# A hybrid encoder layer: the first two projection blocks in turns of 256 tokens, their weights loaded between the first tiles of x, and the sums of squares of kk later in their block

## The chip, the cores and the metric

The kernel runs on one core of one Trainium2 chip. The metric is the device time of one execution in microseconds (us), the median over several runs. The core has five engines with a queue each: TensorE (PE, matrix products, with its own row PEld for loading the stationary operand), VectorE (DVE), ScalarE (ACT), GpSimd (POOL) and SyncE (SP), which here issues the DMA transfers. An engine takes its instructions in the order in which the program gave them.

## The reference, cut to what matters

One layer runs on 1024 prompt tokens and 256 sample tokens of width 1024, so on T = 1280 tokens in all, in float32:

```
u = rmsnorm(x, norm_mix_pre)
(hc, b_gate, c_gate, r, k, v, zf, zb, gd, gate_conv, gate_rwkv) = split(u @ w_in)
y_conv = (b_gate * conv3(c_gate * hc)) @ w_branch_a
kk = k * k_k ; kk = kk / max(norm(kk per head), 1e-12)
for d, z in ((forward, zf), (backward, zb)):
    z = z + shift_mu[d] * (z_shifted - z) ; zw, za = z[:64], z[64:]
    w = exp(-exp(-softplus(-(decay_w0 + tanh(zw) @ decay_w2)) - 0.5))
    a = sigmoid(iclr_a0 + za @ iclr_a2)
    outs[d] = scan over tokens of a 64x64 state per head (r, w, kk, kk*a, kd(k, a), v)
y = groupnorm(outs[0] + outs[1]) + bonus(r, k, r_k, v)
y_rwkv = (y * (sigmoid(gd) @ gate_g2)) @ w_branch_b
x = x + rmsnorm((sigmoid(gate_conv)*y_conv + sigmoid(gate_rwkv)*y_rwkv) @ w_out)
x = x + rmsnorm(conv_ffn(rmsnorm(x)))
x = x + rmsnorm(sigmoid(x @ w_ple_gate) * (p @ w_ple))
```

The change lies in the first lines: the norm of x, the projections zf, zb and gd of u, and the per-head norm of kk.

## The kernel before

**Split products.** Each float32 operand is kept as a high half (rounded) and a low half (the rest). A product is three matmuls: high by high, high by low, low by high (`mm3`). The high half is a cast on ACT, the low half a subtraction on DVE, or on POOL for the first two blocks of weights. Weights pass through `raw` (two buffers), then `wh` and `wl` (two each).

**First loop (lines 887 to 957).** x comes in ten tiles of 128 tokens. For tile i the loop issues the load of tile i+5; scales tile i+1 on DVE (`scale`: tile, 1/rms, gain, into `xs`); transposes tile i on PE in eight 128x128 pieces into two banks `tp`; casts these into the high half of `U` on ACT and subtracts the low half on DVE; takes the root for tile i+3 (`root`: square root on ACT, reciprocal on DVE, four small steps on POOL) and the squares of tile i+4 (`stats`: ACT squares and sums, POOL scales the sum); and then lets the fill queue run for some us of matrix work with `go`. The low and high halves of the first two blocks' weights are made in the turns i = 2 and 3. The constants' later part, the small vectors and gate_g2 are loaded on the same SP queue in the turns 2 and 6; gate_g2 is split in turn 9.

**Fill queue (class `Fill`).** All projections are blocks of 128 output columns. A block gives units: one unit is the three matmuls of one of eight pieces of the inner dimension, on up to 512 tokens (booked at 0.65 us) or 256 (0.325 us). `go(us)` takes units until their booked time is used up; `until(n)` finishes the first n blocks. The first entry is a `Pair` of the blocks zf and zb, then comes gd, then four times k and r (one pair of heads each), then v, the convolution's and the gates' blocks. When a block has given `ahead` units, the next block's weights are split, one half at each `every` units. After a group of eight units its bank `mm` is evacuated, at the first unit of the group that follows; there are two banks.

**Side jobs.** What follows a block on DVE, ACT and POOL is put on a list by its `done`, and one job is taken from it when units of more than 0.9 us (0.6 us from the k blocks on) have gone by; `run_side()` takes all. zf and zb have nine jobs each (token shift, tanh, cast and low half of zw, cast and low half of za), gd has three (scale, cast, low half). The ten products with gate_g2 (`g_out`) stand in the k block of the first head pair, after `go(3.0)` and `run_side()`, and need gd's halves.

**After the loop (lines 960 to 968)** space of the first loop is taken over by a new pool; two loads of constants go to it and to a buffer `gth`, and ACT casts two tiles (`bo`, `ind`) from them.

**Head pairs (lines 990 to 1002).** For each of four head pairs: in the k block, the small products of the pair before (`rates`: `lora` and what follows on ACT, DVE, POOL, with stores to DRAM in `d_in`); then the r block, where after 1.7 us of units kk squared is split (`halve`) and after a further lead `kk_norm` lets PE sum the squares over the head (`ones`, with `bo`), and DVE takes the maximum, four reciprocals and a product with kk. That product goes into the `rates` of the same pair, in the next k block. After the four pairs the scan begins, which reads `d_in` and `d_kr` back.

All five engines' instructions are pinned to program order by a small wrapper, whose line 199 is therefore the line of nearly all rows.

Of the kernel before, what the change touches and what calls it, by code (L numbers as in the profile page):

```python
# [18 lines left out]
TTS = ((0, 512), (512, 512), (1024, 256))  # L19
# [40 lines left out]
class B:  # L60
# [5 lines left out]
    def sb(self, pool, shape, dt=F32, tag=None, bufs=None):  # L66
        kw = {} if bufs is None else dict(bufs=bufs)
        return pool.tile(shape, dt, name=tag, tag=tag, **kw)
# [57 lines left out]
def build(tc, I, O, dbg=None, upto=99):  # L126
# [5 lines left out]
    def tok(name, i, n=1):  # L132
        if i < 8:
            return I[name + "_prompt"][0, i * 128:(i + n) * 128, :]
        return I[name + "_sample"][0, (i - 8) * 128:(i - 8 + n) * 128, :]
# [24 lines left out]
    def close(*ps):  # L160
        for p in ps:
            open_pools.pop(id(p)).__exit__(None, None, None)
# [47 lines left out]
    PADS = (1, 513, 1027)  # L210
# [6 lines left out]
    def mm3(out, st_, mv, k, last):  # L217
        (sh, sl), (mh, ml) = st_, mv
        PE.matmul(out, sh, mh, start=k == 0, stop=False)
        PE.matmul(out, sh, ml, start=False, stop=False)  # L220
        PE.matmul(out, sl, mh, start=False, stop=k == last)
# [6 lines left out]
    def side(fs):  # L228
        sides.extend(fs)

    def run_side(n=1000, qs=(soon, sides)):
        for q in qs:
            while q and n > 0:
                q.pop(0)()
                n -= 1

    class Block:

        parts, us, ahead, every = 1, 13.0, 4, 4
# [15 lines left out]
        def units(self):  # L255
            hi, lo = self.w
            if self.begin:
                self.begin()
            for (t0, n), po in zip(TTS, PADS):
                ps = sb(pmm, [128, 512], F32, "mm")[:, 0:n]  # L260
                for k in range(8):
                    mm3(ps, (hi[:, k, :], lo[:, k, :]), ucm(t0, n)(k), k, 7)
                    yield n / 512 * 0.65
                self.evac(ps, t0, n, po)
            if self.done:
                self.done()

    class Pair:

        parts, us, ahead, every = 2, 26.0, 36, 2  # L270

        def __init__(self, *blocks):
            self.blocks = blocks
# [7 lines left out]
        def units(self):  # L281
            for x in self.blocks:
                x.begin()
            for p, q in ((0, 0), (1, 0), (0, 1), (0, 2), (1, 1), (1, 2)):
                x, (t0, n), po = self.blocks[p], TTS[q], PADS[q]
                ps = sb(pmm, [128, 512], F32, "mm")[:, 0:n]
                for k in range(8):
                    mm3(ps, (x.w[0][:, k, :], x.w[1][:, k, :]), ucm(t0, n)(k), k, 7)
                    yield n / 512 * 0.65
                x.evac(ps, t0, n, po)  # L290
                if q == 2:
                    x.done()

    class VBlock:

        parts, us, ahead, every = 2, 26.0, 56, 4
# [173 lines left out]
    def ones(ps, w, hl):  # L470

        for t0, n in TTS:
            for q in range(2):
                PE.matmul(ps[:, t0:t0 + n], w, hl[q][:, t0:t0 + n], start=q == 0, stop=q == 1)
# [18 lines left out]
    def kk_norm(hp):  # L493

        ps = sb(psm, [128, 3 * 512], F32, "sm")
        ones(ps, S1["bo"], S1["sq"])
        n2 = kns[hp] = sb(p1, [128, T], F32, "t5", 3)
        V.tensor_scalar(n2, ps[:, 0:T], 1e-24, None, ALU.max)
        side([lambda t=t: V.reciprocal(n2[:, t:t + 320], n2[:, t:t + 320]) for t in range(0, T, 320)])
        side([lambda: V.tensor_tensor(n2, n2, kks[hp], ALU.mult)])  # L500
# [134 lines left out]
    class Branch:  # L635


        parts, us, ahead, every = 1, 6.4, 2, 3
# [45 lines left out]
    class Out:  # L684

        ahead, every = 4, 4
# [165 lines left out]
    fill = Fill(items, left)  # L852
    fill.early[first_out - 2] = 1
    go = fill.run
# [9 lines left out]
    def load_x0(i):  # L864
        if i < NT:
            X0[i] = sb(wq, [128, D], F32, "cvy") if i == 4 else sb(p0, [128, D], F32, "x", 5)
            SP.dma_start(X0[i], tok("x", i))

    def stats(i):
        if i < NT:  # L870
            ss = sb(p0, [128, 1], F32, "ss", 3)
            A.activation(junk, X0[i], AF.Square, accum_out=ss)
            ms = S1["ms", i] = sb(p0, [128, 1], F32, "ms", 3)
            G.tensor_scalar(ms, ss, 1.0 / D, 1e-6, ALU.mult, ALU.add)

    def root(i):
        if i < NT:
            s = S1["s", i] = sb(p0, [128, 1], F32, "s", 3)
            A.activation(s, S1["ms", i], AF.Sqrt)
            S1["rs", i] = b.newton(p0, S1["ms", i], s, 1, f"n0{i % 3}", V if i == 0 else G, V)  # L880

    def scale(i):
        if i < NT:
            S1["xs", i] = sb(p0, [128, D], F32, "xs", 2)
            V.scalar_tensor_tensor(S1["xs", i], X0[i], S1["rs", i], gmix, ALU.mult, ALU.mult)
# [2 lines left out]
    SP.dma_start(cst[:, 0:128], I["consts"][:, 0:128])  # L888
    SP.dma_start(gmix, I["norm_mix_pre"].broadcast_to((128, D)))
    load_x0(1)  # L890
    load_x0(2)
    load_x0(3)
    load_x0(4)
    junk = sb(p1, [128, D], F32, "o5", 4)
    warm = sb(p0, [128, 1], F32, "warm")
    G.memset(warm, 1.0)
    A.activation(warm, warm, AF.Sqrt)
    fill.load_next()
    half = sb(cp, [128, 24], F32, "half")
    lw = []  # L900

# [3 lines left out]
    stats(1)  # L905
    root(1)
    stats(2)
    root(2)
    stats(3)
    for i in range(NT):  # L910
        load_x0(i + 5)
        if i == 1:
            fill.load_next()
        if i == 2:
            SP.dma_start(cst[:, 128:], I["consts"][:, 128:C_EARLY])
            for name, n in (("conv_w", 12), ("conv_b", 4), ("shift_mu", 2), ("decay_w0", 8),
                            ("iclr_a0", 8), ("k_k", 4), ("k_a", 4), ("r_k", 4)):
                ap = I[name]
                flat = ap.rearrange({2: "a b -> (a b)", 3: "a b c -> (a b c)"}[len(ap.shape)])
                SP.dma_start(prow[at:at + n, :], flat.rearrange("(r p) -> r p", p=128))  # L920
                PC[name] = at
                at += n
            pc = lambda name, i: pcol[:, PC[name] + i:PC[name] + i + 1]
        scale(i + 1)
        pss = []
        for j in range(2):
            ps = sb(pt, [128, 4, 128], F32, "tp")
            for k in range(4):
                PE.transpose(ps[:, k, :], S1["xs", i][:, (4 * j + k) * 128:(4 * j + k + 1) * 128], ident)
            uh = U[:, 4 * j:4 * j + 4, 0, i * 128:(i + 1) * 128]  # L930
            A.copy(uh, ps)
            pss.append((ps, uh))
        for j, (ps, uh) in enumerate(pss):
            V.tensor_tensor(U[:, 4 * j:4 * j + 4, 1, i * 128:(i + 1) * 128], ps, uh.bitcast(F32), ALU.subtract)
        root(i + 3)
        stats(i + 4)
        if i in (2, 3):
            for _ in fill.split_next():
                pass
        if i == 6:  # L940
            ps = sb(pt, [128, 4, 128], F32, "tp")
            PE.transpose(ps[:, 0, 0:at], prow[0:at, :], ident[0:at, 0:at])
            V.tensor_copy(pcol[:, 0:at], ps[:, 0, 0:at])
            V.tensor_scalar(half[:, 0:16], pcol[:, PC["decay_w0"]:PC["decay_w0"] + 16], 0.5, None, ALU.mult)
            V.tensor_scalar(half[:, 16:20], pcol[:, PC["k_a"]:PC["k_a"] + 4], 0.5, None, ALU.mult)
            V.tensor_scalar(half[:, 20:24], pcol[:, PC["k_a"]:PC["k_a"] + 4], -0.5, 1.0, ALU.mult, ALU.add)
        if i == 6:
            raw = sb(p0, [128, DC], F32, "sm", 1)
            for par in range(2):
                SP.dma_start(raw[:, par * 256:(par + 1) * 256].rearrange("p (h v) -> p h v", v=64),  # L950
                             I["gate_g2"][0].rearrange("k (h p v) -> p k h v", p=2, v=64)[par])
        if i == 9:
            S1["g2"] = sb(p1, [128, DC], F32R, "g2h"), sb(p1, [128, DC], F32R, "g2l")
            A.copy(S1["g2"][0], raw)
            V.tensor_tensor(S1["g2"][1], raw, S1["g2"][0].bitcast(F32), ALU.subtract)

        go((0, 0, 0, 2.6, 2.6, 2.6, 2.5, 2.6, 2.6, 2.6)[i])
    close(p0)


# [9 lines left out]
    def mix(n, jobs, lead=0.0, used=0.0):  # L970

        go(lead)
        run_side()
        for j in jobs:
            j()
            go((12.6 - lead - used) / len(jobs))
        fill.until(n + 1)
# [16 lines left out]
    for hp in range(4):  # L994
        if hp > 0:
            mix(2 + 2 * hp, rates(hp - 1), 0.9)
        go(1.7)
        if hp > 0:
            bonus(hp - 1)
        side(halve("sq", "kk2"))  # L1000
        mix(3 + 2 * hp, [lambda: kk_norm(hp)], 6.0, 1.7)
    go(1.0)
    for j in rates(3) + [lambda: bonus(3)]:
        j()
# [830 lines left out]
    for g in range(NG - 1):  # L1835
# [3 lines left out]
        for i in range(NT):  # L1839
            down(g, i)  # L1840
            if i in (2, 5):
                n = 2 * g + 2 + (i == 5)
# [177 lines left out]
```

## Time and profile before

| | us |
|---|---|
| median of 3 runs | 2298.47 |
| lowest, highest | 2292.66, 2304.94 |
| profiled execution | 2319.18 |
| its span, first to last instruction | 2317.3 |
| mean granted TensorE clock | 0.975 |

The profiled execution is one run of its own, a little slower than the timed ones; times of day below are microseconds from the start of its span. A row of the timeline names start, duration, engine, line, operation, output, inputs, shapes and count; in brackets stands how long the engine had been idle before it and what ended that. "x2" merges neighbours. A row of the windows names the stretch and its length, then the busy time of PE, PEld, DVE, ACT and POOL with their instruction counts, the granted clock, the share of the DMA engines and GB/s.

### The profile page before, as it was taken

The page shows a single profiled execution, that of the slowest core. Times are in us where ns is not written, and L with a number is a line of the kernel's source. Part 1 is how long each engine was busy: PE and PEld are TensorE (multiplying, and loading weights), DVE is VectorE, ACT ScalarE, POOL GpSimd, SP SyncE. Part 2 cuts the span into 40 slices and gives each one's busy share as a digit, 9 for nine tenths or more (in the row PEclk, how much of TensorE's full clock was granted, in tenths as well). Part 3 has the DMA queues.
Part 4 walks back from the last instruction along what each step waited for, and adds up shares of the span by engine and source line. Part 5 has one row for each costly group of instructions (what it writes and reads, how often), then busy time and mean ns, then how long its engine had stood idle before and what let it go on. Part 6 is the DMA issues. An engine that isn't in the chain of part 4 may idle for free.

```text
span 2317.3 us, 40119 instructions
## 1 busy us (share of the span) xinstructions
PE 2193.0 (95%) x15895; PEld 1883.6 (81%) x15895; DVE 1494.1 (64%) x2402; ACT 853.9 (37%) x1490; POOL 610.9 (26%) x1372
## 2 busy tenths in 40 slices
PE   6999999999998999999999999999999899999998
PEld 5877887777777777788887999999999878887886
DVE  5488645655656776556667677776777845566565
ACT  4533322322233434342244454444445431113444
POOL 3034246756765676500000000000000012115000
PEclk9999999989998999999999999999999999999999
DMA  4356754434455665454424632221221442224111
GB/s 156 114 134 151 158 163 126 129 97 120 117 140 144 170 188 162 126 179 162 166 102 146 191 105 71 69 77 63 77 72 60 136 146 82 82 82 164 50 62 69
DMA packets 333959, 278.58 MB, mean 120 GB/s; under 512 B 93677, under 2 KB 297291, under 8 KB 333771
## 3 DMA queue, kind: packets, MB, share of 16 engines
q1 hardware_dynamic: 333771, 276.01, 40.3%
q8 instruction: 125, 2.05, 0.4%
q14 instruction: 63, 0.52, 0.1%
HBM read 192.50 MB, written 83.44 MB: 119 GB/s over the span
## 4 chain that ended last, share of the span: by engine, by line
PE 56%; DVE 10%; DMA 6%; SPq 3%; issue 2%; POOL 2%; ACT 2%; ACTq 0%; POOLq 0%; DVEq 0%
PE mm L199 24%; PE X L199 12%; PE Y L199 9%; PE g L199 7%; SPq L199 3%; PE p L199 3%; DMA dW<-W 2%; DVE h L199 2%; DMA MT<-dW 1%; POOL W L199 1%; POOL tm L199 1%; DMA dA<-AT 1%; PE y L199 1%; DVE wl L199 1%; DVE AT L199 1%
## 5 line engine op out<-in xcount | busy, mean ns | idle before, releaser
L199 PE MATMUL mm<-U,wh 128*128 128x512 f32 (+1 forms) x1872 | 547.8, 380 | 2.9 <-ACT U L199 2.3
L199 PEld LDWEIGHTS mm<-U,wh 128*128 128x128 f32 x1872 | 329.1, 196 | 64.0 <-ACT U L199 3.2
L199 PE MATMUL mm<-U,wl 128*128 128x512 f32 (+1 forms) x936 | 343.7, 367 | 1.1 <-POOL wl L199 1.1
L199 POOL TENSOR_TENSOR wl<-raw,wh 128x1024 fp32r<-128x1024 f32 x12 | 29.3, 2456 | 996.1 <-ACT wh L199 995.9
L199 POOL TENSOR_TENSOR tm<-W,U 128x60 f32<-128x60 f32 (+24 forms) x620 | 223.7, 361 | 191.1 <-DMA W<-in_consts 79.2
L199 POOL TENSOR_TENSOR W<-W,tm 128x60 f32<-128x60 f32 (+24 forms) x620 | 228.8, 369 | 48.6
L199 PEld LDWEIGHTS mm<-U,wl 128*128 128x128 f32 x936 | 182.9, 195 | 31.0 <-POOL wl L199 1.6
L199 DVE TENSOR_TENSOR f<-f,mm 128x512 f32<-128x512 f32 x200 | 136.4, 687 | 100.9 <-PE mm L199 99.7
L199 PE MATMUL mm<-MG,act 128*128 128x512 f32 x600 | 159.8, 393 | 4.8 <-DVE f L199 4.8
L199 DVE SCALAR_TENSOR_TENSOR h<-MGb,fcol,h 128x255 f32<-128x255 f32 (+1 forms) x176 | 152.6, 880 | 14.4 <-ACT h L199 12.6
L199 PE MATMUL X<-B,wh 128*128 128x384 f32 (+1 forms) x936 | 157.4, 314 | 2.3 <-DVE MGb L199 2.3
L199 ACT CAST wh<-raw 128x512 fp32r<-128x512 f32 (+1 forms) x142 | 114.9, 810 | 102.7 <-PE Y L199 41.6
L199 PEld LDWEIGHTS X<-B,wh 128*128 128x128 f32 x936 | 143.4, 188 | 2.8 <-DVE MGb L199 2.8
L199 PE MATMUL X<-B,wl 128*128 128x384 f32 (+1 forms) x804 | 137.1, 315 | 4.9 <-DVE MGb L199 3.7
L199 PEld LDWEIGHTS mm<-MG,act 128*128 128x128 f32 x600 | 113.2, 189 | 29.3 <-DVE f L199 5.2
L199 PEld LDWEIGHTS X<-B,wl 128*128 128x128 f32 x804 | 123.7, 190 | 5.3 <-DVE MGb L199 3.9
L199 PE MATMUL mm<-wh,MG 128*128 128x512 f32 x400 | 126.3, 394 | 0.0
L199 PE MATMUL g<-WG,MG 128*128 128x512 f32 x480 | 112.8, 391 | 0.0
L199 PEld LDWEIGHTS g<-WG,MG 128*128 128x128 f32 x480 | 89.5, 188 | 18.2
L199 DVE TENSOR_TENSOR wl<-raw,wh 128x1024 fp32r<-128x1024 f32 (+1 forms) x67 | 78.0, 1165 | 25.2 <-ACT wh L199 24.8
L199 PEld LDWEIGHTS mm<-wh,MG 128*128 128x128 f32 x400 | 74.8, 187 | 18.5
L199 PE MATMUL Y<-B,wh 128*128 128x384 f32 x420 | 85.1, 335 | 0.0
(495 smaller groups left out, 4285.1 us busy)
## 6 DMA issues: line engine op xcount, KB each, us to landing
raw<-in_w_up SPq DMA_DIRECT2D x54, 512.0 KB
raw<-in_w_in SPq DMA_DIRECT2D x39, 512.0 KB
X<-d_in SPq DMA_DIRECT2D x20, 772.0 KB
d_act<-h SPq DMA_DIRECT2D x22, 640.0 KB
MGb<-d_act SPq DMA_DIRECT2D x20, 640.0 KB
raw<-in_w_down SPq DMA_DIRECT2D x22, 512.0 KB
d_in<-o SPq DMA_DIRECT2D x16, 640.0 KB
X<-d_kr SPq DMA_DIRECT2D x20, 512.0 KB
```

What stands on the lines that cost most here:

```text
L199: return lambda *a, **k: tc.keep_in_program_order(f(*a, **k))
```

## The change

Four things are edited, and nothing of what is computed.

1. `Pair` goes through its two blocks in ten groups of 256 tokens, zf and zb in turn, where it went through six groups (512, 512, then 512 and 256 of zf, 512 and 256 of zb). zf is done after the ninth group and zb after the tenth. The next block's weights are split from unit 73 of 80 on, not from unit 36 of 48.
2. The loads of the two blocks' weights are issued after x1 and after x2, not after x4 and in turn 1. Their halves are made in the turns 0 and 1, not 2 and 3; each of these two steps also issues the next weights' load on SP.
3. The squares of tile i+3 and the root of tile i+2 are taken in turn i, one tile later than before. The fill queue takes one group of eight units in each turn from turn 1 on; before, it started in turn 3.
4. In the r block the lead ahead of `kk_norm` is 8.6 us, not 6.0.

```diff
     class Pair:
-        parts, us, ahead, every = 2, 26.0, 36, 2
+        parts, us, ahead, every = 2, 26.0, 73, 2
...
         def units(self):
             for x in self.blocks:
                 x.begin()
-            for p, q in ((0, 0), (1, 0), (0, 1), (0, 2), (1, 1), (1, 2)):
-                x, (t0, n), po = self.blocks[p], TTS[q], PADS[q]
+            for q in range(10):
+                p, t0, n = q % 2, q // 2 * 256, 256
+                x, po = self.blocks[p], PADS[min(t0 // 512, 2)] + t0 % 512
                 ps = sb(pmm, [128, 512], F32, "mm")[:, 0:n]
                 for k in range(8):
                     mm3(ps, (x.w[0][:, k, :], x.w[1][:, k, :]), ucm(t0, n)(k), k, 7)
                     yield n / 512 * 0.65
                 x.evac(ps, t0, n, po)
-                if q == 2:
+                if q > 7:
                     x.done()
...
     load_x0(1)
+    fill.load_next()
     load_x0(2)
+    fill.load_next()
     load_x0(3)
     load_x0(4)
...
-    fill.load_next()
...
     stats(2)
-    root(2)
-    stats(3)
     for i in range(NT):
         load_x0(i + 5)
-        if i == 1:
-            fill.load_next()
...
-        root(i + 3)
-        stats(i + 4)
-        if i in (2, 3):
+        root(i + 2)
+        stats(i + 3)
+        if i < 2:
             for _ in fill.split_next():
                 pass
...
-        go((0, 0, 0, 2.6, 2.6, 2.6, 2.5, 2.6, 2.6, 2.6)[i])
+        go(0 if i == 0 else 2.59)
...
-        mix(3 + 2 * hp, [lambda: kk_norm(hp)], 6.0, 1.7)
+        mix(3 + 2 * hp, [lambda: kk_norm(hp)], 8.6, 1.7)
```

## The prediction

> **What bounds the kernel now.** I read the page's head and its chain first, then the timeline of the first 60 us, then windows over the later steps, then the rows of single waits.
>
> ```profile
> span 2317.3 us, 40119 instructions
> PE 2193.0 (95%) x15895; PEld 1883.6 (81%) x15895; DVE 1494.1 (64%) x2402; ACT 853.9 (37%) x1490; POOL 610.9 (26%) x1372
> PE 56%; DVE 10%; DMA 6%; SPq 3%; issue 2%; POOL 2%; ACT 2%; ACTq 0%; POOLq 0%; DVEq 0%
> ```
>
> TensorE (PE) is busy 95% of the span and has most of the chain. The change leaves its matrix work the same in columns, so a gain must come from PE's idle or slow time. The timeline of the start (start, duration, engine, operation; in brackets the idle time before it and what ended that):
>
> ```profile
> 17.85 1.94 PE L199 MATMUL tp<-cst,xs 128*128 128x128 f32 x8 [0.94 <-DVE xs L199]
> 24.41 1.52 PE L199 MATMUL mm<-U,wh 128*128 128x512 f32 x2 [1.80 <-ACT U L199]
> 24.56 2.37 POOL L199 TENSOR_TENSOR wl<-raw,wh 128x1024 fp32r<-128x1024 f32 x1
> 26.99 0.80 PE L199 MATMUL mm<-U,wl 128*128 128x512 f32 x1 [1.05 <-POOL wl L199]
> 30.14 1.05 PE L199 MATMUL mm<-U,wh 128*128 128x512 f32 x2
> 34.11 0.62 PE L199 MATMUL mm<-U,wh 128*128 128x512 f32 x2
> ```
>
> Until 24.41 PE does only transposes. Its third matmul waits for the low half of the weights, which GpSimd (POOL) splits off in 2.37. Of each pair, 0.39 warm and some 0.62 cold is the pipeline of the last one, so a 512-column matmul advances PE by 0.43 at 30.14 (cold) and by 0.23 at 34.11 (warm). Late start, cold clock and a 1 us wait are what an earlier start could win.
>
> The next windows give a stretch, its length and the busy time of PE, PE's weight loads, VectorE (DVE), ScalarE (ACT) and POOL:
>
> ```profile
> 0.00:20.00 20.00, 5.88 (x24) 4.56 (x24) 8.44 (x17) 10.73 (x23) 6.18 (x23) 1.00 0.88 296
> 47.86:51.51 3.65, 3.65 (x21) 3.08 (x20) 1.29 (x2) 1.07 (x2) 0.00 (x0) 1.00 0.00 0
> 51.51:56.35 4.84, 4.26 (x34) 3.82 (x33) 3.55 (x5) 2.08 (x4) 0.00 (x0) 1.00 0.13 18
> 64.78:78.81 14.03, 14.03 (x75) 11.93 (x73) 9.11 (x9) 9.25 (x10) 0.00 (x0) 1.00 0.32 90
> 110.69:153.94 43.25, 38.47 (x181) 29.82 (x180) 36.26 (x20) 14.78 (x16) 15.13 (x6) 0.98 0.60 135
> 153.94:196.84 42.90, 38.37 (x181) 29.80 (x181) 36.70 (x20) 14.99 (x16) 15.17 (x6) 0.98 0.62 146
> 196.84:239.85 43.01, 39.70 (x181) 30.74 (x181) 40.12 (x22) 15.96 (x17) 15.19 (x6) 0.94 0.69 146
> ```
>
> 47.86 to 51.51 is one turn of the first loop: eight transposes and 12 matmuls of 512 columns on old tokens. 51.51 to 56.35 is the last turn: 24 matmuls of 256 columns on the tile just transposed, 4.84 because they wait for its copies. 64.78 to 78.81 is the gd block. The last three are the head-pair periods, from one norm of kk to the next: 43 each, though PE is busy in only 38 to 40. The rows of DVE, ACT and PE say why:
>
> ```profile
> 153.94 1.49 DVE L199 TENSOR_SCALAR t<-sm 128x1280 f32<-128x1280 f32 x1 [1.03 <-PE sm L199]
> 185.35 3.60 DVE L199 TENSOR_SCALAR kk<-k,pcol 128x1280 f32<-128x1280 f32 x1
> 188.98 1.28 ACT L199 ACTIVATE t<-kk 128x1280 f32<-128x1280 f32 x1 [7.82 <-DVE kk L199]
> 192.47 1.25 ACT L199 CAST gl<-t 128x1280 fp32r<-128x1280 f32 x1
> 193.83 1.49 DVE L199 TENSOR_TENSOR t<-t,gl 128x1280 fp32r<-128x1280 f32 x1 [4.88 <-ACT gl L199]
> 196.84 1.49 DVE L199 TENSOR_SCALAR t<-sm 128x1280 f32<-128x1280 f32 x1 [0.39 <-PE sm L199]
> 284.01 1.04 ACT L199 CAST ZL<-raw 128x1024 fp32r<-128x1024 f32 x1 [10.57 <-DMA d_in<-o]
> 285.59 0.39 PE L199 MATMUL mm<-wh,U 128*128 128x256 f32 x1 [1.32 <-ACT gth L199]
> ```
>
> The norm feeds DVE at 153.94. DVE then works through its queue to kk (185.35 to 188.95), ACT squares and casts until 193.72, DVE makes the low half until 195.32, PE sums, and the next norm starts at 196.84. So this is a **ring of DVE and ACT**; PE only waits in it. The last period ends the same way: at 284.01 ACT, and at 285.59 PE through ACT, have waited for the last store of that ring. What delays the ring's first turn at 110.69 delays all that follows.
>
> **The change, part by part.** *Start.* The two weight loads of 512 KB are issued between x1, x2 and x3. At the 296 GB/s of the first 20 us each pushes what is behind it on SP's queue by 1.8: x2 by one, x3 and x4 by two. x3's squares sit on ACT ahead of the first cast of weights; I put x3 at 15.5 (bounds 13.4 to 17). Then the cast ends at 17.7, POOL's split (2.37, behind a scaling on DVE that holds it off until 18.3) at 20.7, and the third matmul starts there instead of at 26.99. Twenty-two matmuls of 256 columns at half of 0.43 end at 25.4. PE is warm some 5 us after 20.7, as it was after 26.99.
>
> From there the turns alternate: those with an own tile cost 4.84 and now there are four (turns 3, 5, 7, 9) where before only two were left after 26.99; the others cost 3.7. The second turn costs 4.2 as it is half cold, the sixth 3.9 with the small transpose in it. So the last turn starts at 25.4 + 4.2 + 4.84 + 3.7 + 4.84 + 3.9 + 4.84 + 3.7 = 55.4, against 51.51: **+3.9**, with more of the pair done by then. Before, gd began 13.27 after the last turn did (64.78): 4.84 of that turn and 8.43 for two further groups. Now one group of 24 x 0.119 = 2.9 is left, so gd would begin 7.7 after 55.4, at 63.1: without a new wait a gain of 1.7.
>
> *The wait that takes its place.* ACT's queue holds the casts of the constants:
>
> ```profile
> 53.97 0.68 DVE L199 TENSOR_TENSOR g2l<-sm,g2h 128x512 fp32r<-128x512 f32 x1
> 59.10 0.30 ACT L199 CAST bo<-gth 128x128 fp32r<-128x128 f32 x1 [4.86 <-DMA gth<-in_consts]
> 59.68 1.05 ACT L199 CAST wh<-raw 128x1024 fp32r<-128x1024 f32 x1
> 60.76 1.23 DVE L199 TENSOR_TENSOR wl<-raw,wh 128x1024 fp32r<-128x1024 f32 x1 [0.52 <-ACT wh L199]
> ```
>
> Their load can only start when the space of the first loop is free (after 53.97) and lands at 59.10, 7.6 after the last turn began. Behind it on ACT come the evacuation and the gd block's weights, ready at 61.99, which the old order's 8.4 of work covered. Now that cover is 2.9. At 55.4 + 7.6 = 63.0 ACT goes on, the weights are split at 66.0, and gd starts as if at 65.6 (two matmuls run before): **+0.8** against 64.78. Bounds: -1.7 if the constants land earlier, +2 if the loop is 1.2 slower.
>
> *The side jobs.* Block zf is done after group 8 and zb after 9, where before zf was done 24 units before the pair's end. By the counting rule of the queue (one job after 0.9 us of units) eight and a fraction more jobs were out before: zb's five last jobs now fall into the k block, behind ACT's last evacuation of gd. Then three jobs of gd follow.
>
> ```profile
> 78.62 1.49 DVE L199 TENSOR_TENSOR za<-o,za 64x1280 fp32r<-64x1280 f32 x1 [0.29 <-ACT za L199]
> 80.14 0.84 DVE L199 TENSOR_SCALAR t<-t 128x1280 f32<-128x1280 f32 x1
> 81.02 1.26 ACT L199 CAST k<-t 128x1280 fp32r<-128x1280 f32 x1 [1.63 <-DVE t L199]
> 82.31 1.49 DVE L199 TENSOR_TENSOR gl<-t,k 128x1280 fp32r<-128x1280 f32 x1 [1.33 <-ACT k L199]
> 83.86 0.50 PE L199 MATMUL tp<-g2h,gl 128*128 128x512 f32 x1 [0.77 <-DVE gl L199]
> ```
>
> From gd's end to the first product with gl took 5.05 (78.81 to 83.86). Now the serial chain there is evacuation 0.4, tanh 1.3 (as the cast of 1.26), cast 1.3, the next weights' cast 1.05, cast 1.3, low half 1.49, and 0.84 + 1.26 + 1.49 of gd: 10.4. PE has five units of 0.7 to put beside it. **+5.35**, with PE idle for some 5.4. Bounds: 0, if the jobs keep up, and +6.4.
>
> *Clock.* An idle stretch at the norm shows what follows:
>
> ```profile
> 109.34 0.39 PE L199 MATMUL sm<-gl,bo 128*128 128x512 f32 x1
> 150.23 0.50 PE L199 MATMUL sm<-gl,bo 128*128 128x512 f32 x1 [2.31 <-ACT gl L199]
> 151.83 0.80 PE L199 MATMUL sm<-t,bo 128*128 128x512 f32 x1 [1.10 <-DVE t L199]
> 153.70 1.05 PE L199 MATMUL mm<-U,wh 128*128 128x512 f32 x2
> 155.79 0.63 PE L199 MATMUL mm<-U,wh 128*128 128x512 f32 x2
> ```
>
> After 3.4 of idleness the matmuls from 151.83 to 155.56 take 3.7 where the warm 0.23 would give 2.1. The longer stall at g_out costs the same: **+1.6**. The gd gap of 2.7 is bounded by 0 and 1.6; I take 0, since it is shorter than this one. The Trainium skill (TensorE: Matmul & The Clock Gate, "Why this matters for your kernels") advises no gaps over about 3 us between bursts; by it the 2.31 gap should have left the clock up, and the trace shows it down at 151.83 with a second gap of 1.10 behind it. By the rule the gd gap costs nothing, by the row up to 1.6, so 2308.5 or 2310.1.
>
> *The sums later in the r block.* 2.6 more of lead is four units, 12 matmuls of 0.23: 2.8. At the first head pair nothing was waiting (109.34 has no bracket), so the ring's first turn starts 2.8 later, **+2.8**. At the other three PE's work from norm to norm is unchanged, and so is the ring; PE waits as before. After the last norm PE has 2.8 less to do, but there it waits for the ring's store (284.01), so nothing comes back except an estimated **-0.5** where the ring waited for PE's later products. Bounds: -11.5 (below) and +2.8.
>
> *The rest* (ten groups instead of six, 240 weight loads instead of 144): at 256 columns weight load and product overlap, as in the turn of 4.84; inside the numbers above.
>
> Sum: 0.8 + 5.35 + 1.6 + 2.8 - 0.5 = **+10.1**. The profiled execution lasted 2319.2, 1.9 more than its span; it would become 2329.3. It is 0.9% above the median of the runs, 2298.47; 10.1 us on that is **2308.5**.
>
> **Rivals.** A measurement of this kernel can tell about 0.5%, 11.5 us, from no change.
> - *The sums pay as a stall removed, and the start pays.* If the ring had slack, the 2.8 of extra cover would take the 6.6 of waits for gl away, and three cold spells of 1.6: -11.4; with gd 1.7 earlier and jobs in time, 2285.4. For it: PE's three waits are real. Against: kk leaves DVE without a gap, and the periods are equal to 0.4.
>
> ```profile
> PE sm L199 <- ACT gl L199: 6.6, 3, 2.6
> ```
>
> - *Only the sums pay*, the start costs its 7.75: 2294.8. This one decides as soon as the second period falls under 43.
> - *Only the start pays.* Constants and jobs come in time: -1.7, then +2.8 and -0.5: 2299.1. It needs the k block's first products to find gl ready, as if ACT had no queue.
> - *A starved start.* x3 at 17 or later and POOL and DVE in each other's way push the loop by 3, and the gd gap turns the clock down: 2313 to 2318 (10.1 + 3 + 1.6 on 2298.5 is 2313.2; the upper end, an estimate, doubles the 3 and adds a second cold spell). For it: DMA is 88% busy in the first 20 us.
> - *The matmuls don't come earlier*, because the weights land behind x as before: the start's terms vanish, only +2.8 stays: 2301, counted with the third.
>
> **How the numbers follow.** Forecast 0.57, own range 2303 to 2314; both pay 0.14; only the sums 0.06; only the start 0.12; starved 0.11. Slower by over 0.5% means above 2310: a third of the forecast (0.19) and nearly all of the starved case, 0.29. Faster means below 2287: three quarters of both pay, 0.11. No change is left with 0.60. The range 2292 to 2315 leaves out the first rival and the starved case's end.
>
> **What would show it.** First matmul on U near 18.3 and the third near 20.7; last turn near 55.4; the cast of bo 7.6 behind it and an idle PE ahead of gd; five jobs of zb between gd's end and the first g_out, PE idle there for 5 and cold after; first norm near 121.5; periods still 43; PE's waits for gl at the three later norms still there. It is wrong if the periods shrink, if g_out waits under 2, or if the first norm comes before 110.

## The result, and the profile after

The median went from 2298.47 to 2315.78 us over five runs each, a ratio of 1.0058 with a 95% interval of 1.0035 to 1.0081: slower by 17.3, where 10.1 was forecast. Timed a second time beside other kernels (below), the same change gave 2310.87 against 2302.22, 1.0036 [1.0022, 1.0049], slower by 8.7. Single executions of one kernel on one chip spread by 18 us (2293.56 to 2311.58 in 34 runs of the kernel before), so a mark inside the trace is the sharper measure. I use two: the first norm of kk, and the point where the first work behind the four head pairs gets its data from the ring's last store (**the ring's end**, 284.01 before). The changed kernel's rows for them, from the timeline:

```profile
121.78 0.39 PE L199 MATMUL sm<-gl,bo 128*128 128x512 f32 x1
123.13 1.49 DVE L199 TENSOR_SCALAR t<-sm 128x1280 f32<-128x1280 f32 x1 [5.00 <-PE sm L199]
294.15 1.05 ACT L199 CAST ZL<-raw 128x1024 fp32r<-128x1024 f32 x1 [9.21 <-DMA d_in<-o]
```

The first norm is 12.44 late (121.78 against 109.34, both without a wait of PE), and the ring's end 10.14 (294.15 against 284.01). The sum in the prediction was 10.05. Each mark comes from one profile of each kernel; the second profile of the changed kernel (below) has 292.85, so 8.84 late, and a kernel that leaves everything up to the first norm as before (8.6 at the last three, below) has 284.32 where before has 284.01. The page of the changed kernel says nothing of this:

```profile
span 2318.6 us, 40314 instructions
PE 2190.1 (94%) x15991; PEld 1887.9 (81%) x15991; DVE 1493.0 (64%) x2402; ACT 853.6 (37%) x1494; POOL 611.5 (26%) x1372
PE 64%; DVE 13%; DMA 9%; POOL 5%; issue 3%; SPq 3%; ACT 3%; ACTq 0%; DVEq 0%; POOLq 0%
```

This execution's span, 2318.6, is only 1.3 above that of before: the profiled run of before was one of its slower ones, and the scan, which the change doesn't touch, took less in the profile after. Its first and last transposes of `Dm` stand at 361.25 and 979.38, 618 apart, against 350.50 and 977.39, 627 apart, before. So the rest is told by stretches ahead of the scan.

**The start.** The timeline of PE after:

```profile
18.32 1.31 PE L199 MATMUL mm<-U,wh 128*128 128x256 f32 x2 [2.15 <-ACT U L199]
20.63 0.58 PE L199 MATMUL mm<-U,wl 128*128 128x256 f32 x1 [1.00 <-POOL wl L199]
24.21 0.52 PE L199 MATMUL mm<-U,wh 128*128 128x256 f32 x2
54.80 1.04 PE L199 MATMUL tp<-cst,xs 128*128 128x128 f32 x8
```

The first matmul on U stands at 18.32 and the third at 20.63, as forecast (18.3, 20.7). The steps between are right too: x3 is there at 15.70, ACT's cast of the weights ends at 17.78 and POOL's split at 20.57 (forecast 15.5, 17.7, 20.7). The clock is up some 3.6 after the third matmul, and the last turn starts at 54.80 (forecast 55.4). The granted clock of the windows doesn't show this first cold stretch: it reads 1.00 from 20.63 to 24.20, though a matmul of 256 columns advances PE by 0.21 there (21.44 to 21.65) and by 0.12 after it (24.56 to 24.68). At the start the rows of PE have to be read, not that column.

**Ahead of gd** ACT waits for the constants' load, and PE for ACT:

```profile
62.45 0.30 ACT L199 CAST bo<-gth 128x128 fp32r<-128x128 f32 x1 [5.15 <-DMA gth<-in_consts]
64.14 0.73 PE L199 MATMUL mm<-U,wh 128*128 128x512 f32 x2 [1.50 <-ACT wh L199]
65.40 0.80 PE L199 MATMUL mm<-U,wl 128*128 128x512 f32 x1 [0.53 <-DVE wl L199]
68.55 0.76 PE L199 MATMUL mm<-U,wh 128*128 128x512 f32 x2
80.62 0.62 PE L199 MATMUL mm<-U,wh 128*128 128x512 f32 x2
```

The cast of `bo` comes 7.65 after the last turn began. PE idles 1.50 and 0.53 and is then cold: the windows after (stretch, length, busy time of PE, PEld, DVE, ACT, POOL, granted clock, DMA share, GB/s) show half the clock in both places where PE had stood still:

```profile
65.40:68.55 3.15, 3.15 (x7) 2.48 (x8) 3.10 (x4) 2.33 (x2) 0.00 (x0) 0.50 0.56 154
90.36:96.60 6.24, 5.95 (x15) 4.18 (x14) 1.99 (x2) 1.17 (x2) 0.00 (x0) 0.54 0.19 63
```

Seven matmuls in 3.15 are 1.5 more than 7 x 0.23. So gd ends at 80.62, 1.81 after the 78.81 of before.

**Ahead of g_out.** The same timeline, now ACT, DVE and PE in turn:

```profile
81.23 1.27 ACT L199 ACTIVATE o<-o 64x1280 f32<-64x1280 f32 x1
82.54 1.26 ACT L199 CAST zw<-o 64x1280 fp32r<-64x1280 f32 x1
83.71 1.04 ACT L199 CAST wh<-raw 128x1024 fp32r<-128x1024 f32 x1
83.88 0.40 PE L199 MATMUL mm<-U,wl 128*128 128x512 f32 x1
84.76 1.25 ACT L199 CAST za<-o 64x1280 fp32r<-64x1280 f32 x1
86.04 1.49 DVE L199 TENSOR_TENSOR za<-o,za 64x1280 fp32r<-64x1280 f32 x1 [0.72 <-ACT za L199]
87.56 0.84 DVE L199 TENSOR_SCALAR t<-t 128x1280 f32<-128x1280 f32 x1
88.44 1.26 ACT L199 CAST k<-t 128x1280 fp32r<-128x1280 f32 x1 [2.42 <-DVE t L199]
89.73 1.49 DVE L199 TENSOR_TENSOR gl<-t,k 128x1280 fp32r<-128x1280 f32 x1 [1.32 <-ACT k L199]
89.79 0.77 PE L199 MATMUL tp<-g2h,k 128*128 128x512 f32 x1 [5.52 <-issue]
91.27 0.79 PE L199 MATMUL tp<-g2h,gl 128*128 128x512 f32 x1 [0.29 <-DVE gl L199]
```

tanh, cast, the next weights' cast, cast, low half, and gd's three: link by link the chain that the prediction wrote down, 10.65 from gd's end to the first product with gl (80.62 to 91.27) where before it was 5.05. PE ends its five units at 84.28 (83.88 + 0.40) and stands 5.52. The profile names no releaser for this wait ("issue"); that the product waits for gd's cast `k`, its input, follows from the times: the cast ends at 89.70, the product starts at 89.79.

**The ring.** The three periods after, and PE's waits in the first 300 us (total, times, longest):

```profile
123.13:165.49 42.36, 38.49 (x182) 30.54 (x181) 36.31 (x20) 14.77 (x16) 15.14 (x6) 0.96 0.51 126
165.49:209.03 43.54, 39.84 (x182) 31.81 (x181) 36.47 (x21) 14.98 (x16) 15.13 (x6) 0.92 0.61 153
209.03:251.11 42.08, 38.38 (x183) 30.59 (x182) 40.38 (x21) 15.94 (x17) 15.18 (x6) 0.96 0.61 142
```

```profile
PE sm L199 <- ACT o L199: 13.0, 4, 3.9
PE tp L199 <- issue: 5.5, 1, 5.5
```

Before, PE's waits ahead of products into `sm` were the 6.6 for `gl` and these two:

```profile
PE sm L199 <- DVE t L199: 4.8, 6, 1.5
PE sm L199 <- ACT o L199: 1.1, 1, 1.1
```

The periods sum to 127.98, against 129.16 before. PE's three waits for `gl` at the norm are gone, as the lead was meant for, and so are those for `t`. In their place PE waits 13.0 at `lora`'s last products (`sm<-za,lw1h`), so about as much as the 12.5 of before. It waits for ACT to empty `sm` into a buffer `o`, and by the row of ACT it has waited there itself, for a store from such a buffer:

```profile
144.60 1.33 ACT L199 ACTIVATE o<-sm,half 128x1280 f32<-128x1280 f32 x1 [9.34 <-DMA d_in<-o]
```

### The profile page after: what moved, and what is told of

It reads as the page before. It is cut to its first block, busy times and chain, and to the rows that moved or that the text cites. A ratio compares the mean times of both kernels' runs of the same rounds, so it can differ in the third digit from the quotient of the medians.

```text
span 2318.6 us, 40314 instructions
## 1 busy us (share of the span) xinstructions
PE 2190.1 (94%) x15991; PEld 1887.9 (81%) x15991; DVE 1493.0 (64%) x2402; ACT 853.6 (37%) x1494; POOL 611.5 (26%) x1372
## 4 chain that ended last, share of the span: by engine, by line
PE 64%; DVE 13%; DMA 9%; POOL 5%; issue 3%; SPq 3%; ACT 3%; ACTq 0%; DVEq 0%; POOLq 0%
PE mm L199 30%; PE X L199 12%; PE Y L199 9%; PE g L199 7%; SPq L199 3%; PE p L199 3%; POOL W L199 2%; DVE t L199 2%; POOL tm L199 2%; DMA dW<-W 2%; DVE h L199 2%; DMA MT<-dW 1%; DMA dA<-AT 1%; PE tp L199 1%; DMA d_in<-o 1%
## 5 line engine op out<-in xcount | busy, mean ns | idle before, releaser
L199 PEld LDWEIGHTS mm<-U,wh 128*128 128x128 f32 x1936 | 336.4, 195 | 65.2 <-ACT U L199 4.5
L199 POOL TENSOR_TENSOR W<-W,tm 128x60 f32<-128x60 f32 (+24 forms) x620 | 233.8, 377 | 48.6
L199 PEld LDWEIGHTS mm<-U,wl 128*128 128x128 f32 x968 | 188.8, 195 | 29.7 <-POOL wl L199 1.3
L199 DVE SCALAR_TENSOR_TENSOR h<-MGb,fcol,h 128x255 f32<-128x255 f32 (+1 forms) x176 | 152.5, 880 | 14.5 <-ACT h L199 12.6
L199 PEld LDWEIGHTS g<-WG,MG 128*128 128x128 f32 x480 | 89.4, 188 | 18.3
```

The source lines that it names most:

```text
L199: return lambda *a, **k: tc.keep_in_program_order(f(*a, **k))
```

## The experiments

My theory had five terms: gd a little late behind the constants, the side jobs' chain at g_out, cold clock after it, 2.8 once for the sums, and a ring of DVE and ACT that neither gives back nor adds anything. The rivals: that the sums pay by taking PE's waits away, that one cause stands behind both gaps of PE, and that the new start pays once its costs are gone.

### The sums' lead alone

The kernel before, with one number changed: at all head pairs, at the last three, or less of it at the first.

```diff
-        mix(3 + 2 * hp, [lambda: kk_norm(hp)], 6.0, 1.7)
+        mix(3 + 2 * hp, [lambda: kk_norm(hp)], 8.6, 1.7)                  # lead_all
+        mix(3 + 2 * hp, [lambda: kk_norm(hp)], 8.6 if hp else 6.0, 1.7)   # lead_later
+        mix(3 + 2 * hp, [lambda: kk_norm(hp)], 6.0 if hp else 4.0, 1.7)   # lead_first_less
```

> The kernel before with the lead ahead of the norm at 8.6 instead of 6.0 in all four head pairs, nothing else. Ring theory: the first norm comes 2.8 us later (DVE's maximum at 113.5 instead of 110.69), the three periods stay at 43, the ring's end (ACT's first cast of the scan's buffers, 284.01 before, 294.15 with the whole change) comes at about 286.5, and PE's waits do not vanish but move from the norm to the product before it that waits for ACT. Rival, that PE's waits at the norm are what costs time: the ring's end at 272 to 276, the time 8 to 11 us lower.

> The kernel before with the lead of 8.6 in the second to fourth head pair only. Ring theory: first norm at 110.69 as before, ring's end within 1 of 284, time as before; PE's waits at the three later norms are moved, not saved. Rival, waits at the norm cost time: ring's end 7 to 11 earlier.

> The kernel before with the lead of the first head pair at 4.0 instead of 6.0 (three units of 0.7 fewer ahead of the norm), the others at 6.0. Ring theory: the first norm is bound by PE's order, not by its data, so DVE's maximum comes 2.1 earlier, near 108.6, and the ring's end near 282; time 2 lower, which the timing can hardly tell. Rival, PE's waits count: no gain, since the norms' waits stay.

Measured (the norm by DVE's row, 110.69 before):

| | first norm | ring's end | ratio to before |
|---|---|---|---|
| before | 110.69 | 284.01 | |
| 8.6 at all | 114.02 | 288.54 | 1.0011 [0.9988, 1.0035] |
| 8.6 at the last three | 111.05 | 284.32 | 0.9979 [0.9952, 1.0005] |
| 4.0 at the first | 108.19 | 281.40 | 0.9982 [0.9958, 1.0007] |

The median times can't tell these apart; the marks can. The lead costs at the first head pair: +3.3 there, and with 2.0 less of it the norm comes 2.5 earlier and the ring ends 2.6 earlier. With 8.6 at all four the ring ends 4.5 later, 2.0 beyond the expectation, so 1.2 more than the first norm explains. At the last three the lead moves the ring's end by 0.3, though it does to PE's waits what it did in the changed kernel. The waits of the kernel with 8.6 at the last three:

```profile
PE sm L199 <- ACT o L199: 11.1, 4, 4.2
PE sm L199 <- DVE t L199: 1.5, 3, 0.9
```

The 6.6 at `gl` went, and `o` rose from 1.1 to 11.1. The sum is the same: 12.6 here, 12.5 before. So the ring sets how long PE stands, and the lead chooses where. Neither ring's end, 284.32 or 288.54, comes near the 272 to 277 of the rival in which the sums pay, and that excludes it. The 0.3 is a balance, though: +0.36 at the first norm, +1.17 in the three periods (130.33 in sum) and -1.22 behind the fourth norm. In the last two periods the granted clock is 0.92 (0.98 and 0.94 before), and DVE waits 1.31 and 2.69 for PE's sums at the third and fourth norm (0.39 and 1.03 before). So here PE, cooled behind one longer wait, does hold up the ring a little.

### The new start alone

The changed kernel with the lead back at 6.0.

```diff
-        mix(3 + 2 * hp, [lambda: kk_norm(hp)], 8.6, 1.7)
+        mix(3 + 2 * hp, [lambda: kk_norm(hp)], 6.0, 1.7)
```

> The change with the lead put back to 6.0, so the new start alone. Ring theory: first norm 2.8 earlier than with the whole change, DVE's maximum at about 120.3 (9.6 after that of the kernel before), PE idle for 5.5 ahead of the first product with gate_g2, ring's end at about 292 (8 later than before), time about 8 us above before. Rival, that the start pays and only the later sums cost: ring's end at or below 284.

First norm 120.54, ring's end 293.22, median 2315.98, 1.0025 [1.0001, 1.0049]. The kernel before, timed beside it, had 2309.09, so the start alone costs 6.9 by time. Against the changed kernel the norm is 2.6 earlier: the sums' term again. The rest of the delay, 9.85 at the first norm, is the start's, so nothing of it pays. At the ring's end the 2.6 is not to be found: 293.22 lies 1.2 beyond the expectation, between the two profiles of the changed kernel (294.15, and 292.85 below). On the new start the sums' term is thus shown at the first norm only.

### The whole change again

> The whole change once more, on the chip of the runs beside it. Ring theory: ring's end (ACT's first cast of the scan's buffers) again near 294, 10 later than in the profile of before, and the rest of the program unchanged, so a time 10 above before, a ratio of 1.0044; what the first timing showed beyond that was the spread of the later stages. Rival: the scan behind it is longer too, by 7 us, ratio 1.0058 or more again.

First norm 123.00, ring's end 292.85, median 2310.87, 1.0036 [1.0022, 1.0049]. The norm repeats to 0.13; the ring's end is 1.3 earlier than in the first profile.

### The constants' casts behind gd's block

The kernel with the new start alone, with the two casts moved behind `fill.until(2)`, so that nothing of gd waits for the constants.

```diff
     for nm, t in (("bo", blocks), ("ind", ind)):
         S1[nm] = sb(p1b, [128, t.shape[1]], F32R, nm)
-        A.copy(S1[nm], t)
...
     fill.until(2)
+    A.copy(S1["bo"], blocks)
+    A.copy(S1["ind"], ind)
```

> The new start with the lead at 6.0, and ACT's two casts of the constants moved behind the gd block, so that nothing on ACT waits for that load. Ring theory: gd starts right behind the pair, near 62.3 instead of 64.9, all that follows is 2.6 earlier than with the start alone; the jobs of zb stay late and PE still idles 5 ahead of the first product with gate_g2; first norm near 117.9, ring's end near 290.5. Rival, that the late jobs are a result of the late constants: the idle time at gate_g2 vanishes as well, first norm near 112.

First norm 116.86, ring's end 288.74, median 2305.03, 1.0006 [0.9992, 1.0021]. PE's gap ahead of gd is gone, and the norm comes 3.68 earlier than with the start alone. The second gap stays as it was:

```profile
63.75 0.62 PE L199 MATMUL mm<-U,wh 128*128 128x512 f32 x2
87.26 0.76 PE L199 MATMUL tp<-g2h,k 128*128 128x512 f32 x1 [5.82 <-issue]
88.74 0.80 PE L199 MATMUL tp<-g2h,gl 128*128 128x512 f32 x1 [0.29 <-DVE gl L199]
```

The first row is gd's first product: no idle time ahead of it, and it runs warm (0.62 for the pair; behind the gap, the pair at 65.99 took 1.05), so the gap was what turned the clock down there. It starts 1.45 after the expected 62.3, of which 0.87 is a later last turn in this profile (56.07, where the start alone has 55.20). gd's end moves from 80.86 to 77.78, by 3.1, and the products with gate_g2 by 2.78 (from 90.04 and 91.52). PE still waits 5.82 there. So the side jobs are a cause of their own, and one cause for both gaps is excluded. The other 0.90 of the 3.68 comes behind that wait, where 12 matmuls took 4.16 here and 5.06 with the start alone: a shorter cold spell. Whether the constants have to do with that, the runs don't show.

### The side jobs taken earlier

On top of that, one job is taken for every 0.6 us of units of the first two entries, not 0.9.

```diff
+    fill.pace = 0.6
     fill.until(2)
```

> As the kernel with the casts moved, and the side jobs taken one per 0.6 us of units already from the end of the first loop, so that those of zf and zb are out before gd ends. Ring theory: no idle time above 1.5 ahead of the first product with gate_g2, first norm near 108.2, 2.5 before that of the kernel before, ring's end near 281.5; time 2.5 below before. Rival, that the groups of 256 tokens cost time by themselves: first norm at 111 or later.

The stall at g_out is gone, but the first norm comes at 113.65 and not at 108.2. A new wait stands at the k block's first matmul:

```profile
78.11 1.26 ACT L199 CAST zw<-o 64x1280 fp32r<-64x1280 f32 x1
79.39 1.25 ACT L199 CAST za<-o 64x1280 fp32r<-64x1280 f32 x1
80.67 0.87 ACT L199 ACTIVATE t<-mm 128x512 f32<-128x512 f32 x2
80.91 1.49 DVE L199 TENSOR_TENSOR za<-o,za 64x1280 fp32r<-64x1280 f32 x1
81.32 1.22 PE L199 MATMUL mm<-U,wh 128*128 128x512 f32 x2 [3.25 <-ACT t L199]
84.60 1.49 DVE L199 TENSOR_TENSOR gl<-t,k 128x1280 fp32r<-128x1280 f32 x1 [1.32 <-ACT k L199]
```

The jobs of zb, now ahead of gd's evacuation in ACT's queue, hold that up, and PE has no bank of `mm` for the k block. The chain has changed the place where PE meets it; its last link, the low half of gd, ends at 86.09, 2.6 earlier than in the run above (88.70) but still 2.3 later than before (83.80). By the first norm, 113.65, the condition of the rival (111 or later) is met, but not by its mechanism: PE is through with gd at about 77.9, 0.9 earlier than before (78.81), so the matrix work in groups of 256 tokens, with its earlier start, is not late. What is late is the work behind it. Counted in units of 256 tokens, zf was done with 24 of 80 still to come in the old order, and its nine jobs ran beside zb's products; now 8 are to come, and the jobs of both blocks stand in a row. Ring's end 285.83, median 2298.30, 0.9979 [0.9965, 0.9993] by time; by the mark still 1.8 behind before. The lower time thus comes from behind the last stage that the change touches, or from spread, and doesn't show that the new start pays.

### A shorter ring

The kernel before, with the cast and the low half of kk squared put ahead of ACT's copy of `bn` (and so ahead of the cast of the next weights too).

```diff
-    def bonus(hp):
+    def bonus(hp, first=()):
...
         ones(ps[0:32], S1["ind"], S1["rk"])
+        for j in first:
+            j()
         A.copy(S1["bn"][rows], ps[0:32, 0:T])
...
         if hp > 0:
-            bonus(hp - 1)
-        side(halve("sq", "kk2"))
+            bonus(hp - 1, halve("sq", "kk2"))
+        else:
+            side(halve("sq", "kk2"))
```

> The kernel before, with the cast of kk squared (high half) and the low half given ahead of ACT's copy of the bonus and of the cast of the next weights; nothing else. Ring theory: these two, 1.22 and 1.04, stood between ACT's square and its cast in three of the ring's turns; the periods shrink from 43 to about 40.8, ring's end near 277.5, time 6 to 7 below before. Rival, that DVE's queue alone or PE sets the period: it stays at 43.

Median 2295.72 against 2302.22, 0.9960 [0.9942, 0.9977]: 0.4% less, with the whole interval below 1. The periods, and ACT in the second of them:

```profile
110.73:151.54 40.81, 37.74 (x182) 29.30 (x181) 36.58 (x20) 14.89 (x16) 15.14 (x6) 1.00 0.51 131
151.54:192.62 41.08, 37.82 (x182) 29.33 (x182) 36.81 (x21) 15.09 (x16) 15.17 (x6) 1.00 0.59 156
192.62:234.13 41.51, 38.00 (x183) 29.42 (x182) 37.74 (x22) 16.14 (x17) 15.17 (x6) 1.00 0.65 155
```

```profile
186.56 1.27 ACT L199 ACTIVATE t<-kk 128x1280 f32<-128x1280 f32 x1 [7.91 <-DVE kk L199]
187.87 1.26 ACT L199 CAST gl<-t 128x1280 fp32r<-128x1280 f32 x1
189.16 1.22 ACT L199 COPY bn<-sm 32x1280 f32<-32x1280 f32 x1
190.43 0.50 PE L199 MATMUL sm<-gl,bo 128*128 128x512 f32 x1 [1.67 <-ACT bn L199]
276.74 1.05 ACT L199 CAST ZL<-raw 128x1024 fp32r<-128x1024 f32 x1 [8.73 <-DMA d_in<-o]
```

The cast follows the square at once; before, 2.2 of other work lay between them (190.26 to 192.47). Each period falls to about 41 where 2.2 less gives 40.8, and the ring ends 7.3 earlier: 5.8 of it in the three periods, 1.5 in the stretch behind the fourth norm, which was not forecast. Nothing of PE's work was touched, and taking away PE's waits for `gl` (8.6 at the last three, above) did not shorten the periods; together the two runs show that DVE and ACT set the period. The granted clock in the periods is 1.00 where it was 0.94 to 0.98: PE's wait at this norm is 1.67 now, where it was two in a row, of 2.63 and 1.10. PE is also busy 0.6 to 1.7 less in each period, and the runs don't separate what that adds from what ACT's shorter queue gives.

### Everything together

The shorter ring with 4.0 of lead at the first head pair, on the old start (`ring_and_lead`) and on the new start with both mends (`best`); and the latter with a pace of 0.75 (`best_pace`).

```diff
+        mix(3 + 2 * hp, [lambda: kk_norm(hp)], 6.0 if hp else 4.0, 1.7)
...
-    fill.pace = 0.6
+    fill.pace = 0.75      # best_pace alone
     fill.until(2)
```

> The kernel before, with the shorter ring (cast and low half of kk squared ahead of the cast of the bonus) and with the first head pair's sums after 4.0 of lead; the start is the old one. If the first norm sets all four and the ring sets the period, the two gains add: first norm 110.7 - 2.7 = 108.0, periods 41, end of the ring 276.7 - 2.6 = 274.1, and a median about 10 below before (ratio 0.9955). The rival is that PE, busy 38 to 40 of each period, is the bound once the ring takes 41: then the earlier first norm is given back in PE's waits for the first low halves, and the end of the ring stays at 276.7.

> The changed kernel with everything mended: constants' casts behind gd's block, side jobs of the first pair taken after every 0.6 of units, 4.0 of lead at the first head pair and 6.0 at the others, and the shorter ring. By adding: first norm 113.65 - 2.7 = 110.9, end of the ring 285.8 - 2.7 - 7.3 = 275.8, so 1.7 behind the same kernel with the old start, and a median about 8 below before (ratio 0.9965). A rival that the new start is worth something once its costs are gone would need an end of the ring under 274.

> The same, but the first pair's side jobs are taken after every 0.75 of units instead of 0.6. If the 3.25 that PE waited at 81.3 for ACT came from too many side jobs ahead of gd's evacuation, fewer are in front of it now: that wait falls under 2, no stall of 5 comes back ahead of g_out, and the end of the ring is near 273.5. If two or more jobs of zb fall behind gd again, a wait of 2 to 3 shows at g_out instead, and the end of the ring stays near 275.8.

| | first norm | ring's end | median, before's | ratio |
|---|---|---|---|---|
| old start | 108.90 | 276.27 | 2296.45, 2305.84 | 0.9970 [0.9954, 0.9985] |
| new start, mended | 111.24 | 278.74 | 2295.91, 2305.84 | 0.9974 [0.9952, 0.9995] |
| the same, pace 0.75 | 113.13 | 280.55 | 2303.38, 2305.84 | 0.9989 [0.9970, 1.0008] |

The new start stays behind the old one by 2.5 at the ring's end, so with these two mends that rival is out too; the medians, 2295.91 and 2296.45, don't tell the two apart. Its 278.74 is 2.9 beyond the expectation: the wait of 3.29 ahead of the k block is still there. With a pace of 0.75 the stall of 5.8 at g_out is back and 280.55 is beyond both expectations for that run: between 0.6 and 0.75 PE's wait jumps from the one place to the other, and no pace between them was run. The earlier first norm did not add in full: on the old start the ring ends at 276.27, near the rival's 276.7 and not at 274.1. With the ring at 41, from the first norm to the ring's end took 167.4 to 167.5 in all three kernels against 166.0 with the shorter ring alone. DVE starts the three later norms of each of these profiles without an idle time that ends with PE's sums, so the rival's mechanism, PE holding up the ring, isn't seen there. Since the stretch lay between 169.9 and 174.5 in the nine profiles with the old ring, one run of 166.0 doesn't settle whether the 1.4 is spread. Three of the kernels (the shorter ring alone, and the first two of this table) are ahead of both the kernel before and the changed one, by the ratio of the times and at the ring's end; among themselves their intervals overlap.

## Why the prediction was right, and where it was not

The changed kernel is slower for the reasons given. That the ring's end is late by the amount given (10.14 measured, 10.05 in the sum) is luck: up to the first norm the change cost 1.9 more than the sum has, and behind it 1.8 came back beyond the -0.5 of the sum. The median of the first timing, 2315.78, lies 7.3 above the forecast and 0.8 above the upper end of the range, and its 0.58% is over the line at 0.5%, to which I had given 0.29; the second timing, 0.36%, is under it, where I had put 0.60. Their intervals overlap; the marks in the trace (10.1 and 8.8 late) speak for the second. By steps:

| step | forecast | measured | from |
|---|---|---|---|
| gd's start and end | +0.8 | +1.81 | 80.62 against 78.81 |
| side jobs at g_out | +5.35 | +5.60 | 10.65 against 5.05 |
| cold clock, then the lead | +1.6, +2.8 | +5.03 | 91.27 to 121.78 against 83.86 to 109.34 |
| first norm | +10.55 | +12.44 | sum |
| from there to the ring's end | -0.5 | -2.3 | 171.02 against 173.32 |
| ring's end | +10.05 | +10.14 | |

*Start.* Right: both matmuls to 0.1, the last turn 0.6 early. *The wait that takes its place.* Right in its place and its cause (7.65 against 7.6). What failed is the size, by the clock: I had taken 0 of 0 to 1.6 for the gap ahead of gd, because it was shorter than the one at the norm. It cost 1.5, the upper bound, and without it gd would end 0.3 late. The Trainium skill (TensorE: Matmul & The Clock Gate, "Why this matters for your kernels") asks for no gaps over about 3 us. The trace shows that less can do: 1.50 and 0.53 around two matmuls left a granted clock of 0.50. The row of the profile, though of another place, was the better guide.

*The side jobs.* Right, and shown by two experiments: it stays when the constants are out of the way, and it goes when the jobs are taken earlier. What the prediction didn't see is that taking them earlier moves much of PE's wait to another place (5.82 ahead of g_out, then 3.25 ahead of the k block): the chain has lost the cover of 16 units of the pair. By this reading the start of the chain would have to move, not its pace; no run tried that. *Clock* at g_out: some 2.3 rather than 1.6, for 12 matmuls from 91.27 to 96.37 took 5.1 and not 2.8; PE had stood 5.5 here and 3.4 in the row that I took.

*The sums later in the r block.* The 2.8 holds at the first norm (3.3 on the old start, 2.6 on the new), and is paid once at the first head pair. That PE waits in the ring and doesn't set it is right but for the two late sums of PE in the kernel with 8.6 at the last three. The step's sentence that PE would wait at the later norms "as before", and the last part's that its waits for gl would still be there, are **wrong**: they are gone, and 13.0 at `lora` stand in their place. The ring sets how long PE stands, and the prediction took it to set the place too. It had no price here, since the sum of PE's waits is nearly the same (12.5 before, 13.0 after).

*The tail.* -0.5 was forecast and -2.3 measured, 171.02 and 169.85 in the two profiles of the change. Of the -2.3, 1.18 lie in the three periods and 1.12 behind the fourth norm (44.16 before, 43.04 after). The prediction let PE wait for the ring's store behind the last norm. In the profile before it doesn't: PE is busy in 44.16 of these 44.16 (41.26 of 43.04 after), and waits only the 1.32 at 285.59. But 44.16 is the longest of the thirteen profiles (42.14 to 43.57 in the others), and with 8.6 of lead on the old start the whole stretch was 174.5, so the lead doesn't give the time back by itself. What does is open; the stretch differs by up to 4.7 among profiles with the same ring.

## What to carry to other kernels

A wait of the busiest engine inside a period that another ring sets is hardly a cost: moving the work around it moved the wait here, and only a shorter link of the ring (a cast queued behind two other instructions that could wait) shortened the period. Finishing two blocks together, instead of one after the other, makes their follow-up work on the other engines come all at once; before blocks are interleaved, count what that work will still have to run beside. And where executions spread by more than the effect, a mark in the trace behind the edit and ahead of the noisy stage tells what the medians can't.

## What was not expected of the hardware

**How little it takes to turn the clock down.** 1.50 and 0.53 with two matmuls between them did it (0.50 above). The single wait at each of the three later norms of the shorter ring (1.67 in the one shown) did not: its periods ran at 1.00. And after a longer one the fall can come late. In the changed kernel's timeline:

```profile
145.98 0.85 PE L199 MATMUL sm<-za,lw1h 128*128 128x512 f32 x3 [3.87 <-ACT o L199]
146.75 0.97 PE L199 MATMUL sm<-za,lw1l 64*128 64x512 f32 x3
188.19 1.38 PE L199 MATMUL sm<-za,lw1h 128*128 128x512 f32 x3 [3.70 <-ACT o L199]
231.71 0.85 PE L199 MATMUL sm<-za,lw1h 128*128 128x512 f32 x3 [3.70 <-ACT o L199]
232.48 1.30 PE L199 MATMUL sm<-za,lw1l 64*128 64x512 f32 x3
```

After 3.87 and one of the waits of 3.70 the first three products still run warm (0.85) and the next slow down; after the other wait of 3.70 the first are slow already (1.38). The same wait thus costs a different amount, by when it falls; none of the runs shows what sets that.

**The spread of the scan.** From the first to the last `Dm` took 611 to 627 in the thirteen profiles of this case, though the scan's code is the same in all. It hides effects of a few us in any single time, and I don't know its cause.
